# Scores of a pair's two heads issued side by side in the banded attention and both memory attentions

## The chip, the cores and the metric

One core of one Trainium2 chip. The metric is the device time of one execution in microseconds. TensorE (PE) multiplies, VectorE (DVE), ScalarE (ACT) and GpSimd (POOL) work on tiles, SyncE (SP) issues most transfers. PSUM, where products land, has eight banks here, all taken by one kind of tile (`ps`, 128 x 512).

## What is computed

The reference is two blocks on 512 positions of 1024 features, all in float32. The first has a gated long convolution, a chunked mLSTM with 4 heads and a feed-forward. The second has two layers, each followed by a feed-forward: layer A (keys chosen by an indexer, then latent attention) and layer B (banded attention). Both layers add memory attention. Only these matter here, cut down:

```python
B_HEADS, B_KV_HEADS, B_HEAD_DIM, B_WINDOW = 16, 4, 64, 128
MEM_LEN, MEM_HEADS, MEM_HEAD_DIM = 256, 4, 64

# layer B: query i sees keys j with 0 <= i - j < 128; four query heads share a key/value head
s = einsum('bnqhgd,bnkhd->bnhgqk', qb, kk) * scale
s = where(mask, s, NEG_INF)
m = maximum(max(s, -1), sk)                # sk: a learned sink of each head
p = exp(s - m[..., None])
p = p / (sum(p, -1) + exp(sk - m))[..., None]
o = einsum('bnhgqk,bnkhd->bnqhgd', p, vv)

# memory attention, in both layers, 256 keys
s = einsum('bshd,bmhd->bhsm', q, k) * MEM_HEAD_DIM ** -0.5
o = einsum('bhsm,bmhd->bshd', softmax(s, -1), v)
x = x + concatenate([mix, mem_o], -1) @ w_out
```

## The kernel before

Every product is done as three TensorE matmuls of rounded parts (high x high, high x low, low x high), in the function `mm3` (lines 356 to 358). An operand's parts are made by a cast on ScalarE (L347) and a subtraction on VectorE (L348); weights by a cast on ScalarE (L337) and a subtraction on VectorE or GpSimd (L340).

A head has 64 dims, so two heads share the 128 partitions: head e = 0 is in rows 0 to 63, head e = 1 in rows 64 to 127. A score product uses 64 rows of TensorE. In layer B, `pairs_b` is called for each half of the 16 heads: four pairs, eight heads. For one head, `first` makes four score pieces (128 queries by 128 or 256 keys) in two `ps` tiles and then the softmax: VectorE adds the mask and takes the maximum (L1600, one for each piece), joins the sink (L1604), ScalarE does four exponentials (L1607) and the sink's (L1610), VectorE adds and inverts (L1611, L1613), GpSimd scales four pieces (L1615). `second` transposes seven pieces of 128 x 128 (L490) into two `ps` tiles, splits them (`pt`, L347 and L348), multiplies with the values (`head_out`, L1179 to L1186 and `mm3`) into one `ps` tile for the pair, and splits that after the pair's second head. `mem_attn` does the same for four heads with 256 keys: two tiles of scores for a head, reduce (L1206), exponentials (L1213, two for a tile), reciprocal (L1216), scaling (L1219).

The order of the code is written by generators. `pipe(n, first, second, ahead)` runs `first` for `ahead` heads (3 in `pairs_b` and in layer A's memory attention, 1 in layer B's), then `second` of a head and `first` of a later one in turn. `weave` mixes the steps of such a chain with those of a projection: in layer B's first half with the queries of the second half and the memory queries (1.2 steps for each), in the second half, where `both` also mixes `pairs_b` and `mem_attn`, with the output projection `b_wo` (0.4 steps). From that code a scheduler makes the final order of each engine's instructions; an engine works through its own in order.

Of the kernel before, what the change touches and what calls it, by code (L numbers as in the profile page):

```python
# [8 lines left out]
ALU = mybir.AluOpType  # L9
# [26 lines left out]
# ---------------------------------------------------------------- host layout  # L36
# [179 lines left out]
# ---------------------------------------------------------------- the kernel  # L216
class Net:
# [17 lines left out]
    # ---- tiles  # L235
# [20 lines left out]
    # ---- background work, mixed in between weight units: chains of steps, two at a time  # L256
# [15 lines left out]
    # ---- order of emission: pieces of matrix products go between the steps of dependent chains  # L272
# [7 lines left out]
    def weave(self, g, fill, rate=1.0):  # L280
        """Steps of g, each followed by `rate` steps of fill; then the rest of fill."""
# [14 lines left out]
    def pipe(self, n, first, second, ahead=2):  # L296
        """first(i) runs ahead of second(i, what first returned)."""
# [8 lines left out]

    def both(self, a, b):
        """Two steps of a, one of b, and so on."""
# [120 lines left out]
    # ---- norms  # L429
# [16 lines left out]
    def colsum(self, *parts, nb=NB):  # L446
        """Sums over partitions and parts, as columns [position, block]."""
# [7 lines left out]
    def rstd(self, src, n, count, tag="rstd"):  # L455
        """1/sqrt(src/count + EPS) on columns."""
# [15 lines left out]
    def bcast(self, rc, nb=NB, out=None):  # L472
        """Columns [s, block] to a tile [any partition, s]."""
# [18 lines left out]
    # ---- prologue  # L492
    def setup(self):
# [17 lines left out]
        # has the table of the square root loaded in time  # L511
# [27 lines left out]
    def rope_tables(self):  # L539
# [6 lines left out]
        for rot in (32, 16):  # L546
# [13 lines left out]
            # whichever way the conversion rounds, the rest comes into [-pi, pi]  # L560
# [28 lines left out]
    def gain(self, o, k, g):  # L589
        """(1 + scale) * g of a norm, as a column."""  # L590
# [11 lines left out]
    def mod_norm(self, k, bc, aff, shift):  # L602
        """rms_norm(x) * g * (1 + scale) + shift, as two parts."""
# [28 lines left out]
    def conv31(self, out, a, i):  # L632
        """The long convolution, with its input in PSUM."""
# [16 lines left out]
    def block1(self):  # L650
# [28 lines left out]
        # the first n-tiles go along with the modulation, feature tile by feature tile  # L679
# [125 lines left out]
    def gates(self, h):  # L805
        """Input and forget gates: the running maximum of i - F, its columns, and exp(-m)."""
# [35 lines left out]
    def values1(self, h, c):  # L842
        """v of two heads, with a column of ones behind each."""
# [39 lines left out]
    def scores1(self, hd, qk, g):  # L883
# [6 lines left out]
        # where the weights of key block j are: j = 0 | j = 1, 3 | j = 2  # L890
# [219 lines left out]
    def mem_proj(self, layer):  # L1110
        """Keys [2 heads x 64, 256] and values [256, heads], as two parts."""
# [76 lines left out]
    def mem_attn(self, qm, ahead=3):  # L1188
        """qm: 2 x ([128, s] hi, lo)."""
        nc = self.nc  # L1190
        keys, vals = self.mem
        outs = []

        def first(i):
            pr, e = i // 2, 1 - i % 2
            r = slice(64 * e, 64 * e + 64)
            pes = []
# [490 lines left out]
```

## Time and profile before

| | us |
|---|---|
| median of three runs | 2231.48 (2231.43 to 2233.22) |
| span of the profiled execution | 2231.4 |
| layer A, stretch of the memory attention | 1033.5 to 1092.5 |
| layer B, banded and memory attention | 1671.7 to 1818.2 |
| last feed-forward | 1818.2 to the end |

The profile is of one execution; its span is 0.08 us below the median of the runs, inside their spread. Busy time counts an instruction from its start to its end, and TensorE's matmuls overlap each other, so distances from start to start tell more there. A wait is shown with the instruction that released it.

### The profile page before, as it was taken

Reading aid. Unit: us, or ns where it says so; the run is one execution under the profiler, and the core shown is the slowest. Engines: PE = TensorE matmul, PEld = TensorE weight load, DVE = VectorE, ACT = ScalarE, POOL = GpSimd, SP = SyncE. Lnnn points to the kernel's source line nnn. Section 1 sums busy time; section 2 is a strip of 40 time slices with the busy share of each in tenths; the row PEclk is TensorE's granted clock in tenths of the full one; section 3 lists DMA queues with packets and bytes.
Section 4 is the critical chain, followed back from the end, with each engine's and each line's share of the span. In section 5 each row is a group of like instructions: output and inputs, shape, how many; then the busy total and the mean of one; then the engine's idle time right before and its main releaser. Section 6 shows DMA issues by size and latency. Waiting matters only on the chain.

```text
span 2231.4 us, 28798 instructions
## 1 busy us (share of the span) xinstructions
PE 2170.9 (97%) x9988; PEld 1752.3 (79%) x9988; DVE 1367.6 (61%) x2677; ACT 996.3 (45%) x1856; POOL 531.2 (24%) x518
## 2 busy tenths in 40 slices
PE   6999999989999999998999999999999999999998
PEld 4888888867788888876778888888887778888886
DVE  8887967596733333669985654545556665545354
ACT  4655457724422323545464432323545645323233
POOL 3554454552000000242451210101133321101010
PEclk9999999999999999999999999999999999999999
DMA  7322222283422222221211222222321012222222
GB/s 264 105 86 81 93 83 90 92 276 126 157 95 95 95 95 95 97 79 43 67 57 62 99 94 94 94 95 94 118 86 53 33 48 90 94 95 94 95 94 88
DMA packets 120534, 216.91 MB, mean 97 GB/s; under 512 B 13762, under 2 KB 18114, under 8 KB 120388
## 3 DMA queue, kind: packets, MB, share of 16 engines
q1 hardware_dynamic: 120388, 215.08, 28.8%
q8 instruction: 78, 1.28, 0.2%
q14 instruction: 68, 0.56, 0.1%
HBM read 212.93 MB, written 2.10 MB: 96 GB/s over the span
## 4 chain that ended last, share of the span: by engine, by line
PE 87%; DVE 8%; issue 2%; DMA 2%; ACT 1%; SPq 0%; POOL 0%; DVEq 0%; ACTq 0%; POOLq 0%
PE ps L356 28%; PE ps L357 28%; PE ps L358 28%; PE ps L490 2%; DVE big L585 2%; DMA big<-in_ada_dram 1%; DVE bias L1434 1%; DVE m L1433 1%; DVE bias L1396 0%; DVE x L1310 0%; DVE rope L1105 0%; PE ps L451 0%; DVE hs L348 0%; DMA x<-in_xT_dram 0%; PE ps L480 0%
## 5 line engine op out<-in xcount | busy, mean ns | idle before, releaser
L337 ACT CAST wh<-st 128x512 fp32r<-128x512 f32 (+1 forms) x698 | 429.2, 617 | 877.1 <-PE ps L357 592.8
L357 PE MATMUL ps<-hs,wh 128*128 128x512 f32 x1800 | 715.2, 397 | 5.3 <-DVE hs L612 5.1
L358 PE MATMUL ps<-hs,wl 128*128 128x512 f32 x1800 | 712.7, 397 | 7.5 <-DVE wl L340 5.1
L356 PE MATMUL ps<-hs,wh 128*128 128x512 f32 x1800 | 711.4, 399 | 5.7 <-ACT hs L611 5.1
L340 DVE TENSOR_TENSOR wl<-st,wh 128x512 fp32r<-128x512 f32 x488 | 346.7, 712 | 302.3 <-ACT wh L337 299.6
L358 PEld LDWEIGHTS ps<-hs,wl 128*128 128x128 f32 x1800 | 339.3, 188 | 91.6 <-DVE wl L340 7.1
L356 PEld LDWEIGHTS ps<-hs,wh 128*128 128x128 f32 x1800 | 339.2, 189 | 91.3 <-ACT hs L611 8.3
L357 PEld LDWEIGHTS ps<-hs,wh 128*128 128x128 f32 x1800 | 339.2, 188 | 88.5 <-DVE hs L612 7.0
L340 POOL TENSOR_TENSOR wl<-st,wh 128x512 fp32r<-128x512 f32 (+1 forms) x210 | 280.9, 1341 | 360.6 <-ACT wh L337 334.5
L1036 POOL TENSOR_TENSOR t<-t,t 128x512 f32<-128x512 f32 x44 | 69.3, 1576 | 602.5 <-DVE t L1035 533.4
L438 POOL TENSOR_TENSOR t<-t,t 128x512 f32<-128x512 f32 (+1 forms) x51 | 64.3, 1261 | 521.6 <-ACT t L434 520.1
L627 DVE SCALAR_TENSOR_TENSOR big<-ps,vec,big 128x511 f32<-128x511 f32 (+28 forms) x240 | 160.9, 719 | 11.3 <-ACT big L624 11.3
L358 PE MATMUL ps<-big,wl 128*128 128x512 f32 x400 | 157.8, 396 | 2.3 <-POOL wl L340 2.3
L356 PE MATMUL ps<-big,wh 128*128 128x512 f32 x400 | 157.8, 396 | 0.0
L357 PE MATMUL ps<-big,wh 128*128 128x512 f32 x400 | 157.7, 395 | 0.0
L357 PE MATMUL ps<-wl,hs 128*128 128x512 f32 (+1 forms) x320 | 125.3, 392 | 0.0
L358 PE MATMUL ps<-wh,hs 128*128 128x512 f32 (+1 forms) x320 | 124.8, 390 | 0.0
L356 PE MATMUL ps<-wh,hs 128*128 128x512 f32 (+1 forms) x320 | 124.0, 394 | 0.0
L348 DVE TENSOR_TENSOR big<-t,big 128x512 fp32r<-128x512 f32 (+1 forms) x86 | 58.6, 689 | 79.3 <-ACT big L347 77.3
L347 ACT CAST big<-t 128x512 fp32r<-128x512 f32 (+1 forms) x86 | 51.4, 600 | 99.4 <-POOL t L1036 83.7
L358 PEld LDWEIGHTS ps<-big,wl 128*128 128x128 f32 x400 | 75.4, 189 | 21.0 <-POOL wl L340 3.1
L357 PEld LDWEIGHTS ps<-big,wh 128*128 128x128 f32 x400 | 75.5, 189 | 17.9
(324 smaller groups left out, 2970.9 us busy)
## 6 DMA issues: line engine op xcount, KB each, us to landing
st<-in_f_up_dram SPq DMA_DIRECT2D x176, 256.0 KB, 2.6
st<-in_w_up_dram SPq DMA_DIRECT2D x88, 256.0 KB, 2.5
st<-in_f_down_dram SPq DMA_DIRECT2D x88, 256.0 KB, 2.6
big<-in_ada_dram SPq DMA_DIRECT2D x80, 256.0 KB, 5.0
st<-in_w_down_dram SPq DMA_DIRECT2D x44, 256.0 KB, 2.5
st<-in_w_qk_dram SPq DMA_DIRECT2D x32, 256.0 KB, 2.5
st<-in_w_ogm_dram SPq DMA_DIRECT2D x32, 256.0 KB, 2.5
st<-in_w_glu_dram SPq DMA_DIRECT2D x20, 256.0 KB, 2.5
```

What stands on the lines that cost most here:

```text
L337: nc.scalar.copy(wh, st)
L340: eng.tensor_tensor(out=wl, in0=st, in1=wh.bitcast(F32), op=ALU.subtract)
L347: nc.scalar.copy(hi, src)
L348: nc.vector.tensor_sub(lo, src, hi.bitcast(F32))
L356: nc.tensor.matmul(out, lh, rh, start=start, stop=False)
L357: nc.tensor.matmul(out, lh, rl, start=False, stop=False)
L358: nc.tensor.matmul(out, ll, rh, start=False, stop=stop)
L438: (add or nc.gpsimd).tensor_tensor(out=acc, in0=acc, in1=sq, op=ALU.add)
L490: self.nc.tensor.transpose(out, in_, self.ident[:p, :p])
L585: nc.vector.tensor_tensor_reduce(out=st, in0=st, in1=self.siluc[half], scale=1.0, scalar=acc, op0=ALU.mult, op1=ALU.add, accum_out=out)
L627: nc.vector.scalar_tensor_tensor(out=out[:, d:], in0=x[:, :S - d], scalar=w(j), in1=out[:, d:], op0=ALU.mult, op1=ALU.add)
L1036: nc.gpsimd.tensor_tensor(out=b, in0=b, in1=hold["a"], op=ALU.mult)
```

## The change

A new function `mm3_rows` takes the score products of two heads and issues their three matmuls in turn. `first` of `pairs_b` and of `mem_attn` now takes a pair: two `ps` tiles, one for each head, are filled in turn, the reduces follow for both, and after half of the pieces there is a step for the weaving. In `pairs_b` the softmax of both heads then follows, head 1 first. `pipe` with its `ahead` gives way to `pipe2`: scores of pair 0, then for each pair `second` of its head 1, `first` of the next pair, `second` of its head 0. In after, `mm3` is at lines 368 to 370, the transposes at L512, split at L359 and L360, unit at L349 and L352, `mm3_rows` at L376, L378 and L380, the exponentials at L1636 and L1238.

```diff
+    def pipe2(self, n, first, second):
+        st = yield from first(0)
+        for pr in range(n):
+            more = first(pr + 1) if pr + 1 < n else None
+            nxt = None
+            for i in range(2):
+                yield from second(2 * pr + i, st[1 - i])
+                if more and i == 0:
+                    nxt = yield from more
+            st = nxt
...
+    def mm3_rows(self, *prods):
+        nc = self.nc
+        for out, lh, ll, rh, rl in prods:
+            nc.tensor.matmul(out, lh, rh, start=True, stop=False)
+        for out, lh, ll, rh, rl in prods:
+            nc.tensor.matmul(out, lh, rl, start=False, stop=False)
+        for out, lh, ll, rh, rl in prods:
+            nc.tensor.matmul(out, ll, rh, start=False, stop=True)
...
     def pairs_b(...):
-        def first(i):
-            pr, e = i // 2, 1 - i % 2
+        def first(pr):
...
                 if j % 2 == 0:
-                    both = self.t()
-                    sc2 = self.ps()
+                    both = [self.t(), self.t()]
+                    sc2 = [self.ps(), self.ps()]
                 w = slice((j % 2) * 256, (j % 2) * 256 + n)
-                sc = sc2[:, w]
-                self.mm3(sc, q[j][0][r, d], q[j][1][r, d], k[0][r, n0:n0 + n], k[1][r, n0:n0 + n],
-                         True, True)
+                rows = [slice(64 * e, 64 * e + 64) for e in (1, 0)]
+                self.mm3_rows(*((sc2[x][:, w], q[j][0][r, d], q[j][1][r, d], k[0][r, n0:n0 + n],
+                                 k[1][r, n0:n0 + n]) for x, r in enumerate(rows)))
...
+                if j == 1:
+                    yield
+            for x, e in enumerate((1, 0)):
...
-        yield from self.pipe(8, first, second, ahead)
+        yield from self.pipe2(4, first, second)
...
     def mem_attn(...):
...
-        yield from self.pipe(4, first, second, ahead)
+        yield from self.pipe2(2, first, second)
```

The numbers of instructions of each engine stay the same. Up to layer A's memory attention the order of every engine stays too, and again in the last feed-forward.

The order at three places of layer B. First TensorE at the first scores of the first half: `ps_15180` and `ps_15190` (before) are head 1, `ps_15234` and `ps_15244` head 0; in after 15181 and 15219 are head 1, 15182 and 15220 head 0; `big` are keys, `q` queries, `ps_15103` a projection. Before:

```order
L356 MATMUL ps_15180<-big_14966,q_15146 128x128
L357 MATMUL ps_15180<-big_14967,q_15146 128x128
L358 MATMUL ps_15180<-big_14966,q_15147 128x128
L356 MATMUL ps_15190<-big_14966,q_15164 128x256
L357 MATMUL ps_15190<-big_14967,q_15164 128x256
L358 MATMUL ps_15103<-wh_15268,hs_14579 128x512
L358 MATMUL ps_15190<-big_14966,q_15165 128x256
L356 MATMUL ps_15234<-big_14966,q_15146 128x128
L357 MATMUL ps_15234<-big_14967,q_15146 128x128
L358 MATMUL ps_15234<-big_14966,q_15147 128x128
L356 MATMUL ps_15244<-big_14966,q_15164 128x256
L357 MATMUL ps_15244<-big_14967,q_15164 128x256
```

After:

```order
L376 MATMUL ps_15181<-big_14966,q_15146 128x128
L378 MATMUL ps_15181<-big_14967,q_15146 128x128
L380 MATMUL ps_15181<-big_14966,q_15147 128x128
L376 MATMUL ps_15182<-big_14966,q_15146 128x128
L378 MATMUL ps_15182<-big_14967,q_15146 128x128
L380 MATMUL ps_15182<-big_14966,q_15147 128x128
L376 MATMUL ps_15219<-big_14966,q_15164 128x256
L378 MATMUL ps_15219<-big_14967,q_15164 128x256
L380 MATMUL ps_15219<-big_14966,q_15165 128x256
L376 MATMUL ps_15220<-big_14966,q_15164 128x256
L378 MATMUL ps_15220<-big_14967,q_15164 128x256
L380 MATMUL ps_15220<-big_14966,q_15165 128x256
```

One burst of twelve score products stands where a projection's product interrupted it, and a pair's two heads have their tiles filled for the same pieces. Next TensorE at the transposes of pair 1's first head (`t_15287`, `t_15297` before; `t_15335`, `t_15373` after). Before, its own last score product is 64 matmuls ahead of the first transpose; `ps_15546` are scores of later heads, `ps_15374` is values times weights of pair 0, `hs` are queries of the next half:

```order
L356 MATMUL ps_15546<-big_14975,q_15173 128x256
L357 MATMUL ps_15546<-big_14976,q_15173 128x256
L358 MATMUL ps_15546<-big_14975,q_15174 128x256
L357 MATMUL ps_15374<-pt_15451,big_14834 64x256
L358 MATMUL ps_15374<-pt_15450,big_14835 64x256
L356 MATMUL ps_15374<-pt_15454,big_14864 64x256
L490 MATMUL ps_15569<-cst,hs_15484 128x128 x4
L490 MATMUL ps_15578<-cst,t_15287 128x128 x3
L490 MATMUL ps_15578<-cst,t_15297 128x128
L490 MATMUL ps_15579<-cst,t_15297 128x128 x3
```

After; the burst with the last scores of `t_15373` ends 16 matmuls ahead of its first transpose, three transposes of queries and twelve products with values come between, the last six of which are shown:

```order
L368 MATMUL ps_15320<-pt_15450,big_14849 64x256
L369 MATMUL ps_15320<-pt_15451,big_14849 64x256
L370 MATMUL ps_15320<-pt_15450,big_14850 64x256
L1201 MATMUL ps_15320<-pt_15454,big_14879 64x128
L1202 MATMUL ps_15320<-pt_15455,big_14879 64x128
L1205 MATMUL ps_15320<-pt_15454,big_14880 128x128
L512 MATMUL ps_15533<-cst,t_15335 128x128 x3
L512 MATMUL ps_15533<-cst,t_15373 128x128
L512 MATMUL ps_15534<-cst,t_15373 128x128
L512 MATMUL ps_15550<-cst,hs_15484 128x128 x4
L512 MATMUL ps_15534<-cst,t_15373 128x128 x2
L368 MATMUL ps_15559<-pt_15542,big_14834 128x256
```

The distance to a head's scores went from 64 matmuls to 16, and the first product with the transposed weights (`pt_15542`) stands directly behind the transposes. Last, ScalarE at pair 0 of the second half (`t_15981`, `t_15991` before, `t_15981`, `t_16001` after: head 1; `t_16017`, `t_16027` before, `t_15982`, `t_16002` after: head 0; L1213 and L1238: memory attention). Before:

```order
L1607 ACTIVATE t_15981,l_3739_15980<-t_15981,m_3738_15979 128x128
L1607 ACTIVATE t_15981,l_3739_15980<-t_15981,m_3738_15979 128x256
L1607 ACTIVATE t_15991,l_3739_15980<-t_15991,m_3738_15979 128x256 x2
L1610 ACTIVATE es_3744_16006<-m_3738_15979,sk_14621 128x4
L347 CAST hs_15975<-ps_15933 128x512
L1607 ACTIVATE t_16017,l_3747_16016<-t_16017,m_3746_16015 128x128
L1607 ACTIVATE t_16017,l_3747_16016<-t_16017,m_3746_16015 128x256
L1607 ACTIVATE t_16027,l_3747_16016<-t_16027,m_3746_16015 128x256 x2
L1610 ACTIVATE es_3752_16042<-m_3746_16015,sk_14621 128x4
L1213 ACTIVATE t_16080,l_3761_16079<-ps_16069,mx_3760_16076 128x256 x2
L337 CAST wh_16485<-st_16484 128x512
L347 CAST pt_16152<-ps_16143 128x512
```

After:

```order
L1636 ACTIVATE t_16001,l_3748_16021<-t_16001,m_3738_15979 128x256 x2
L1639 ACTIVATE es_3749_16027<-m_3738_15979,sk_14621 128x4
L359 CAST hs_15975<-ps_15933 128x512
L1636 ACTIVATE t_15982,l_3751_16036<-t_15982,m_3739_15980 128x128
L1636 ACTIVATE t_15982,l_3751_16036<-t_15982,m_3739_15980 128x256
L1636 ACTIVATE t_16002,l_3751_16036<-t_16002,m_3739_15980 128x256 x2
L1639 ACTIVATE es_3752_16042<-m_3739_15980,sk_14621 128x4
L1238 ACTIVATE t_16069,l_3757_16068<-ps_16051,mx_3756_16065 128x256 x2
L1238 ACTIVATE t_16080,l_3761_16079<-ps_16052,mx_3760_16076 128x256 x2
L349 CAST wh_16503<-st_16502 128x512
L359 CAST pt_16116<-ps_16107 128x512
```

The cast of head 1's first transposed tile (`pt_16152` before, `pt_16116` after) stands behind one memory piece more.

## Rows read from the trace of the kernel before

**Rows 1.** The page, busy time by engine (part 1) and the chain that ended last (part 4).
```profile
PE 2170.9 (97%) x9988; PEld 1752.3 (79%) x9988; DVE 1367.6 (61%) x2677; ACT 996.3 (45%) x1856; POOL 531.2 (24%) x518
...
PE 87%; DVE 8%; issue 2%; DMA 2%; ACT 1%; SPq 0%; POOL 0%; DVEq 0%; ACTq 0%; POOLq 0%
```

**Rows 2.** Windows: stretch, length, then busy time of each engine, granted clock.
```profile
1033.50:1092.50 59.00, 54.26 (x268) 42.89 (x267) 58.70 (x162) 26.76 (x66) 21.32 (x29) 0.97 0.12 41
1671.70:1818.20 146.50, 143.03 (x851) 114.00 (x849) 92.98 (x297) 84.73 (x258) 47.78 (x88) 1.00 0.12 39
1818.20:1860.00 41.80, 41.80 (x181) 33.51 (x180) 24.63 (x31) 18.84 (x32) 9.09 (x7) 1.00 0.28 92
```

**Rows 3.** Timeline of TensorE: start, duration, line, tile; two score bursts of layer B.
```profile
1709.22 0.40 PE L358 MATMUL ps<-hs,wl 128*128 128x512 f32 x1
1709.54 0.38 PE L356 MATMUL ps<-big,q 64*128 64x256 f32 x1
...
1711.40 0.40 PE L358 MATMUL ps<-hs,wl 128*128 128x512 f32 x1
```

**Rows 4.** Timeline of TensorE, the indexer's scores; x2 are two that start together.
```profile
993.55 0.39 PE L356 MATMUL ps<-big,q 64*128 64x256 f32 x2
...
994.25 0.28 PE L358 MATMUL ps<-big,q 64*128 64x256 f32 x2
```

**Rows 5.** Timeline of TensorE near the end of layer B.
```profile
1805.09 0.28 PE L356 MATMUL ps<-pt,big 128*64 128x256 f32 x1
1805.20 0.28 PE L357 MATMUL ps<-pt,big 128*64 128x256 f32 x1
...
1805.56 0.22 PE L1185 MATMUL ps<-pt,big 128*64 128x128 f32 x1
1805.62 0.28 PE L1186 MATMUL ps<-pt,big 128*128 128x128 f32 x1
...
1808.26 0.39 PE L356 MATMUL ps<-pt,big 128*128 128x256 f32 x1 [1.57 <-ACT pt L347]
1808.48 1.36 PE L490 MATMUL ps<-cst,t 128*128 128x128 f32 x11
1809.60 0.37 PE L357 MATMUL ps<-pt,big 128*128 128x256 f32 x1
```

**Rows 6.** Timeline of TensorE: a head's last score product and its first transpose.
```profile
1729.29 0.28 PE L358 MATMUL ps<-big,q 64*128 64x256 f32 x1
...
1734.10 0.33 PE L490 MATMUL ps<-cst,t 128*128 128x128 f32 x1
```

**Rows 7.** Timeline of VectorE, the same head.
```profile
1729.25 0.42 DVE L1600 CUSTOM_DVE_ANT_0 t<-ps,cst 128x256 f32<-128x256 f32 x1 [0.53 <-PE ps L358]
...
1729.68 0.42 DVE L1600 CUSTOM_DVE_ANT_0 t<-ps,cst 128x256 f32<-128x256 f32 x1
...
1733.33 0.18 DVE L1613 RECIPROCAL rl<-l 128x4 f32<-128x4 f32 x1
```

**Rows 8.** Timeline of ScalarE: the same head, then a memory piece, then a cast.
```profile
1730.86 0.40 ACT L1607 ACTIVATE t<-t,m 128x128 f32<-128x128 f32 x1 [0.39 <-DVE m L1604]
...
1732.75 0.28 ACT L1610 ACTIVATE es<-m,sk 128x4 f32<-128x4 f32 x1
...
1741.45 0.47 ACT L1213 ACTIVATE t<-ps,mx 128x256 f32<-128x256 f32 x1 [3.80 <-DVE mx L1208]
...
1742.37 0.39 ACT L1607 ACTIVATE t<-t,m 128x128 f32<-128x128 f32 x1
...
1749.16 0.59 ACT L347 CAST pt<-ps 128x512 fp32r<-128x512 f32 x1 [0.70 <-PE ps L490]
```

**Rows 9.** Timeline of GpSimd, the same head.
```profile
1733.67 1.74 POOL L1615 TENSOR_SCALAR t<-t,rl 128x128 f32<-128x128 f32 x4 [1.57 <-DVE rl L1613]
```

**Rows 10.** TensorE's wait for the memory queries, then the window behind it.
```profile
1040.55 0.38 PE L356 MATMUL ps<-big,q 64*128 64x256 f32 x1 [2.56 <-DVE t L1251]
...
1041.90:1045.30 3.40, 3.40 (x10) 2.62 (x9) 3.40 (x9) 0.72 (x2) 0.00 (x0) 0.50 0.02 5
```

**Rows 11.** Waits of TensorE in layer B: line, releaser, us, times, longest.
```profile
PE ps L356 <- ACT pt L347: 1.9, 2, 1.6
```

More of the change, by code (lines that the diff above doesn't have):

```diff
@@ L1221, in first @@
-                pes.append(pe)
+                    rows = [slice(64 * e, 64 * e + 64) for e in (1, 0)]
+                    self.mm3_rows(*((scs[n][:, i * MEM:(i + 1) * MEM], qm[pr][0][r, c],
+                                     qm[pr][1][r, c], keys[pr][0][r, :], keys[pr][1][r, :])
+                                    for n, r in enumerate(rows)))
+                for n, e in enumerate((1, 0)):
+                    sc = scs[n]
+                    mx = self.sm(2, "mx2")
+                    nc.vector.tensor_reduce(out=mx, in_=sc.rearrange("p (i m) -> p i m", i=2),
+                                            axis=AX.X, op=ALU.max)
+                    nc.vector.tensor_scalar(out=mx, in0=mx, scalar1=-0.125, scalar2=None,
+                                            op0=ALU.mult)
+                    l = self.sm(2, "l2")
+                    pe = self.t()
+                    for i in range(2):
+                        c = slice(i * MEM, (i + 1) * MEM)
+                        nc.scalar.activation(out=pe[:, c], in_=sc[:, c], func=AF.Exp, scale=0.125,
+                                             bias=mx[:, i:i + 1], accum_out=l[:, i:i + 1])
+                    rl = self.sm(2, "rl2")
+                    nc.vector.reciprocal(rl, l)
+                    for i in range(2):
+                        c = slice(i * MEM, (i + 1) * MEM)
+                        nc.gpsimd.tensor_scalar(out=pe[:, c], in0=pe[:, c], scalar1=rl[:, i:i + 1],
+                                                scalar2=1.0, op0=ALU.mult, op1=ALU.mult)
+                    pes[e].append(pe)
@@ L1222, in first @@
+                if half == 0:
+                    yield
             yield
@@ L1571, in layer_b, with pairs_b @@
         self.run_all(self.proj_out("b_wo", 4, mo + second))
-    def pairs_b(self, q, kT, vs, half, sk, ahead):
+    def pairs_b(self, q, kT, vs, half, sk):
         nc = self.nc
@@ L1578, in pairs_b, with first @@
         hold = {}
-        def first(i):
-            pr, e = i // 2, 1 - i % 2
-            hd = 8 * half + 2 * pr + e
+        def first(pr):
             k = kT[2 * half + pr // 2]
-            r = slice(64 * e, 64 * e + 64)
             d = slice(pr * P, (pr + 1) * P)
-            m4 = self.sm(NB, "m4")
-            l4 = self.sm(NB, "l4")
-            pes = []
+            m4 = [self.sm(NB, "m4") for _ in range(2)]
+            pes = {1: [], 0: []}
             for j in range(NB):
@@ L1603, in first @@
-                pes.append(both[:, w])
-            nc.vector.tensor_scalar(out=m4, in0=m4, scalar1=sk[:, hd:hd + 1], scalar2=-1.0,
-                                    op0=ALU.max, op1=ALU.mult)
-            for j in range(NB):
-                nc.scalar.activation(out=pes[j], in_=pes[j], func=AF.Exp, bias=m4[:, j:j + 1],
-                                     accum_out=l4[:, j:j + 1])
-            es = self.sm(NB, "es4")
-            nc.scalar.activation(out=es, in_=m4, func=AF.Exp, bias=sk[:, hd:hd + 1])
@@ L1611, in first @@
-            nc.vector.tensor_add(l4, l4, es)
-            rl = self.sm(NB, "rl4")
-            nc.vector.reciprocal(rl, l4)
-            for j in range(NB):
-                nc.gpsimd.tensor_scalar(out=pes[j], in0=pes[j], scalar1=rl[:, j:j + 1], scalar2=1.0,
-                                        op0=ALU.mult, op1=ALU.mult)
+                rows = [slice(64 * e, 64 * e + 64) for e in (1, 0)]
+                self.mm3_rows(*((sc2[x][:, w], q[j][0][r, d], q[j][1][r, d], k[0][r, n0:n0 + n],
+                                 k[1][r, n0:n0 + n]) for x, r in enumerate(rows)))
@@ new lines, in first @@
+                for x, e in enumerate((1, 0)):
+                    nc.vector.tensor_tensor_reduce(out=both[x][:, w], in0=sc2[x][:, w], in1=bm,
+                                                   scale=scale, scalar=LOWEST, op0=ALU.add,
+                                                   op1=ALU.max, accum_out=m4[x][:, j:j + 1])
+                    pes[e].append(both[x][:, w])
+                if j == 1:
+                    yield
+            for x, e in enumerate((1, 0)):
+                hd = 8 * half + 2 * pr + e
+                m, l4 = m4[x], self.sm(NB, "l4")
+                nc.vector.tensor_scalar(out=m, in0=m, scalar1=sk[:, hd:hd + 1], scalar2=-1.0,
+                                        op0=ALU.max, op1=ALU.mult)
+                for j in range(NB):
+                    nc.scalar.activation(out=pes[e][j], in_=pes[e][j], func=AF.Exp, bias=m[:, j:j + 1],
+                                         accum_out=l4[:, j:j + 1])
+                es = self.sm(NB, "es4")
+                nc.scalar.activation(out=es, in_=m, func=AF.Exp, bias=sk[:, hd:hd + 1])
+                nc.vector.tensor_add(l4, l4, es)
+                rl = self.sm(NB, "rl4")
+                nc.vector.reciprocal(rl, l4)
+                for j in range(NB):
+                    nc.gpsimd.tensor_scalar(out=pes[e][j], in0=pes[e][j], scalar1=rl[:, j:j + 1],
+                                            scalar2=1.0, op0=ALU.mult, op1=ALU.mult)
```

34 lines of the change are left out of this document (6 added, 28 removed).

## The prediction

> **What bounds the kernel now.** Read the page's totals and its chain first, then the stretches, then single rows. TensorE is busy 97% of the span and is 87% of the chain that ended last [rows 1]. The change touches two stretches. In layer A's memory attention (1033.5 to 1092.5 us) VectorE is busy 58.70 of 59.00 us and TensorE 54.26: VectorE sets the end there, with the top-k work of the indexer. In layer B (1671.7 to 1818.2 us) TensorE is busy 143.03 of 146.50 us, VectorE only 92.98 and ScalarE 84.73; behind it the feed-forward keeps TensorE busy 41.80 of 41.80 us [rows 2]. So what layer B wins or loses on TensorE moves the end by the same amount, and what layer A wins on TensorE is hidden by VectorE.
>
> The busy time of rows overlaps (matmuls are pipelined), so I cost by start-to-start distances. A 512-wide product takes 0.232 us; two bursts of three 64-row score products between three such products take 1709.22 to 1711.40, 2.18 us, where 3 x 0.232 + 6 x 0.117 = 1.40 would do: a burst of 64-row products costs 0.39 us on top of its products [rows 3]. A 256-wide product takes 0.117 us, a 128-wide one into 64 columns 0.06, a transpose about 0.105 (eleven in 1.12) [rows 5].
>
> Layer B has, in either kernel, 254 products 512 wide, 144 of 256 and 50 of 128 (0.232, 0.117, 0.0585 us: 78.6), 160 transposes (at 0.109, the distance of single ones: 17.4) and 240 score products (192 of 0.117 and 48 of 0.111: 27.8). Before, the scores lie in 46 bursts (18.0), and 17 pairs of them lie beside each other already (-2.0). That is 139.8 us; the stretch took 146.5. So 6.7 us are waits of TensorE, the largest one for a cast of ScalarE [rows 11].
>
> **The change part by part.** No product and no step of a softmax is removed; every engine has the same instructions.
>
> *Overlap.* The trace has a place where 64-row products of both row halves stand together: twelve, from 993.55 to 994.25, all in pairs that start together, a pair each 0.117 us [rows 4]. So a pair costs as much as one product. Layer B can have 120 pairs; in the new order 106 fall into one burst, 17 did: 89 x 0.117 = 10.3 us less. Before, the program issued that burst at 993.55 three and three, not in turn, and it overlapped all the same, so I count every pair in a burst.
>
> *Fewer bursts.* 30 where 46 were: 16 x 0.39 = 6.3 us less. Together 16.6 us, all on the path, since TensorE sets the end there.
>
> The Trainium skill ("TensorEngine Tiling (Array Packing)", Key Properties) says that changing the tiling mode drains TensorE. For the 64-row bursts rows 3 agree, with 0.39 us. For tiles of 64 columns they don't: at 1805.56 a product into 64 columns is followed by one into 128 after 0.06 us [rows 5]. By the rule the borders of 64-column tiles, 46 before and 38 after, would count too; at half of 0.39 each the 16.6 us would be 18.2.
>
> *The pipeline.* What is moved is the distance between a head's scores and its transposes. Before, scores ran three heads ahead. Now both heads of a pair get their scores together, and the next pair's scores go between the two heads. What lies between is the softmax: VectorE adds the mask and takes the maximum, ScalarE does four exponentials and the sink's, VectorE inverts the sum, GpSimd scales four pieces, then TensorE transposes.
>
> The trace has the length of that chain for one head with nothing else in the way: last score at 1729.29 (done about 0.2 later), reduces from 1729.25, exponentials from 1730.86 to 1733.03 (2.17 us), reciprocal 1733.33, GpSimd 1733.67, first transpose 1734.10 [rows 6 to 9]: 4.6 us. With two heads in one burst VectorE has two more reduces of 0.43 us ahead of the maximum: 5.5 us for the first head. The second head's exponentials stand behind the first's: 7.7 us. GpSimd gives a scaled piece each 0.44 us (four in 1.74 [rows 9]) where TensorE could transpose two: a head that is waited for costs 1.0 us more until its last piece.
>
> The Trainium skill (same page, PSUM Bottleneck) says that tiling speeds up TensorE but not the emptying of PSUM. Rows 4 and 7 agree: six pairs take 0.7 us, the four tiles they fill take VectorE 1.7. Without the two queued reduces the waits below would be 4 to 5 us less.
>
> Against 5.5 us stands the other work that the order puts between. In layer B's second half, memory attention's exponentials (0.92 us for a half of a head [rows 8]) also stand in ScalarE's queue. The six places with less than 5.5 us (counted in the order of the changed kernel, pieces of which stand in the section on the change):
> - pair 1 of the first half: 12 products of head values and three transposes, 2.1 us: wait 3.4, scaling 1.0, and the first product needs a cast that stands behind the second head's exponentials, 1.0. Together 5.4.
> - pair 3 of the first half: 2.0 us of other work: 3.5 + 1.0, the cast 0.5, then the second head follows at once (7.7 less what has passed, 0.6, and 0.5 of scaling): 6.1.
> - second half, pair 0: 4.3 us: 1.2. Then the product right behind the transposes needs the cast of them (0.59), which stands on ScalarE behind the second head's exponentials (2.2), a split's cast (0.46), two memory pieces (1.8) and a weight cast (0.46). Before it stood there too, but TensorE had other work first. From the end of the first head's exponentials the cast is done after 5.5; TensorE comes there after 2.3: 3.2. Together 4.4.
> - pair 1: 2.7 us: 2.8, two casts ahead 1.0, scaling 0.9: 4.7.
> - pair 2: 4.6 us: 0.9, scaling 0.9, again a cast behind exponentials, 2.2: 4.0.
> - pair 3: 2.6 us: 2.9 + 1.0, cast 0.5, second head 1.0: 5.4.
>
> That is 30.0 us, and 0.8 at the end of the last pair, as before. What stands behind the waiting product on TensorE waits too, since it works in order: weights' products of the output projection most of all. The pairs that are left have 7 to 17 us of other work and wait for nothing. All other engines get slower by it, not busier.
>
> *Layer A.* Its four heads: 49.9 us of TensorE work before, 49.8 after (four bursts become five, more overlap). VectorE bounds the stretch, and its instructions are the same: 0. TensorE idles 4.74 of the 59.00 us [rows 2]; some half of that, 2 us either way, I allow for the order of VectorE's work.
>
> **Sum.** -16.6 + (30.8 - 6.7) = +7.5 us. The profiled execution has a span of 2231.4 us, the median of the three runs is 2231.48: they can be taken as one. 2231.4 + 7.5 = 2239 us.
>
> **Rivals.**
> 1. *Faster: the waits stay near those of before.* Evidence for it: the head of rows 6 had 3.7 us of other work ahead of its transposes and cost a wait of only about 1.2, and the longest wait of layer B for a cast was 1.6 us [rows 11]; while TensorE waits, the others catch up. If the chain stays 4.6 us and neither casts nor scaling bite, the six places cost 2.5 + 2.6 + 0.3 + 1.9 + 0 + 2.0 = 9.3 us: -16.6 + 9.3 - 6.7 = -14.0, 2217 us. Against it: the two reduces and the exponentials are in the queue's order ahead of the casts and cannot be passed.
> 2. *About the same.* The chain is 5.5 us and scaling counts, but the casts find ScalarE free: 4.4 + 5.1 + 2.1 + 3.7 + 1.8 + 4.4 = 21.5; -16.6 + 21.5 - 6.7 = -1.8: 2230 us.
> 3. *Slower, the clock falls.* After a wait of 2.56 us at 1040.55 (for the memory queries) the granted clock was 0.50 for 3.4 us from 1041.90 [rows 10], that is 1.2 GHz for 2.4. Such a stretch costs up to 1.7 us. Of the waits above four are over 2.8 us; three or four falls give +6: 2245 us. It counts from the first wait that is about as long as that one; the wait of 1.57 us at 1808.26 [rows 5] had no fall behind it, since layer B's clock is 1.00 [rows 2].
> 4. *The change does not do what it says: the halves don't overlap.* Then only 6.3 us are won, and the same waits come: 2239 + 10.3 = 2249 us. Against it: rows 4.
>
> **How the numbers follow.** Likeliest is the sum with its waits, 2239 us: 0.34. Clock on top 0.10, no overlap 0.06: with these, slower by over 0.2% (4.5 us; about what a measurement of this kernel can tell from no change) has 0.50. Rival 2: same, 0.22. Rival 1: faster, 0.28. The range reaches from rival 1 (2217) to rival 4 (2249), which leaves out gains of over 14 us (about 0.1) and several falls of the clock on top of all waits (under 0.1). For the cases slower alone it would be 2236 to 2250.
>
> **What would show it.** In the profile after, layer B's score products start in pairs, as those of rows 4, and there are 30 bursts of them; if they start 0.117 us apart one by one, rival 4 holds. TensorE's waits in layer B for GpSimd's scaled pieces (the transposes) and for ScalarE's casts sum to about 30 us where they were some 3 in that view; near 10 means rival 1. TensorE's busy time in layer B falls, and the stretch is longer than 146.5 us. The granted clock in layer B was 1.00; 0.50 in stretches of 3.4 us means rival 3. Layer A ends where it did, within 2 us. I would be wrong if the second pair's scores or the output projection fill more of the six places than the order shows, or if ScalarE's queue empties faster than 2.2 us a head.

## The result, and the profile after

The median of the changed kernel is 2256.86 us (2256.45 to 2260.1) against 2231.66 (2231.43 to 2233.22) for the kernel before, timed beside it: a ratio of 1.0112 [1.0099, 1.0124], 25.2 us slower. The sign is that of the forecast, the size is not: 2239.0 had been named, and 2256.86 lies above the range, 2217 to 2249. The profiled execution has a span of 2258.4 us.

The page of after, its busy time and its chain, to be laid beside [rows 1]:

```profile
PE 2176.7 (96%) x9988; PEld 1756.7 (78%) x9988; DVE 1364.9 (60%) x2677; ACT 996.3 (44%) x1856; POOL 531.1 (24%) x518
...
PE 86%; DVE 8%; ACT 2%; issue 2%; DMA 2%; SPq 0%; POOL 0%; DVEq 0%; ACTq 0%; POOLq 0%
```

TensorE has the same 9988 matmuls and is busy for 5.8 us longer, although more of them overlap. That is the first hint that something beside waits is at work. In the chain ScalarE has 2% where it had 1%. The windows say where (stretch, length, busy time of PE, PEld, DVE, ACT, POOL, granted clock, DMA share, GB/s): layer A's memory attention, layer B, the last feed-forward, as in [rows 2]:

```profile
1037.90:1096.90 59.00, 50.84 (x248) 39.25 (x247) 56.50 (x156) 23.06 (x60) 19.84 (x27) 0.94 0.13 41
1676.30:1845.00 168.70, 146.47 (x852) 116.80 (x851) 91.95 (x297) 84.31 (x258) 46.51 (x88) 0.88 0.10 34
1845.00:1886.80 41.80, 41.80 (x181) 33.51 (x180) 24.52 (x31) 19.05 (x32) 9.08 (x7) 1.00 0.28 94
```

Layer B grew from 146.5 to 168.7 us, the feed-forward behind it is the same. From the start of layer A's memory attention to that of layer B passed 638.2 us before and 638.4 after, so in these two profiles layer A gives and takes nothing. In layer B two numbers moved: TensorE stands idle for 168.70 - 146.47 = 22.2 us (3.5 before), and the granted clock is 0.88 (1.00 before). VectorE, ScalarE and GpSimd have the work they had.

The waits of TensorE in layer B, as a sum (line, releaser, us, times, longest):

```profile
PE ps L512 <- POOL t L1644: 12.7, 5, 3.2
PE ps L368 <- ACT pt L359: 5.7, 3, 2.7
PE ps L369 <- DVE pt L360: 2.5, 2, 2.0
PE ps L368 <- ACT hs L359: 0.7, 1, 0.7
```

and the long ones singly, from TensorE's timeline (the idle time ahead of the instruction, and its releaser, in brackets):

```profile
1697.58 0.38 PE L368 MATMUL ps<-pt,big 128*128 128x256 f32 x1 [1.56 <-ACT pt L359]
...
1701.40 0.58 PE L369 MATMUL ps<-pt,big 128*128 128x256 f32 x1 [1.97 <-DVE pt L360]
...
1710.72 1.35 PE L512 MATMUL ps<-cst,t 128*128 128x128 f32 x5 [2.40 <-POOL t L1644]
...
1742.18 2.06 PE L512 MATMUL ps<-cst,t 128*128 128x128 f32 x7 [3.00 <-POOL t L1644]
...
1761.53 0.58 PE L368 MATMUL ps<-pt,big 128*128 128x256 f32 x1 [2.75 <-ACT pt L359]
...
1781.46 1.60 PE L512 MATMUL ps<-cst,t 128*128 128x128 f32 x5 [3.23 <-POOL t L1644]
...
1804.82 2.06 PE L512 MATMUL ps<-cst,t 128*128 128x128 f32 x7 [1.45 <-POOL t L1644]
...
1808.29 0.58 PE L368 MATMUL ps<-pt,big 128*128 128x256 f32 x1 [1.41 <-ACT pt L359]
...
1828.70 2.06 PE L512 MATMUL ps<-cst,t 128*128 128x128 f32 x7 [2.57 <-POOL t L1644]
```

In order of time these are pairs 0 (two), 1 and 3 of the first half and pairs 0, 1, 2 (two) and 3 of the second. Most releasers are the two that were forecast: scaled pieces of GpSimd ahead of transposes, and casts of ScalarE; at 1701.40 it is a subtraction of VectorE. The durations at the left show the rest: seven transposes take 2.06 us at 1742.18, where eleven took 1.36 in [rows 5], and a 256-wide product 0.58 instead of 0.39. The windows of the six places where the granted clock was low (columns as above):

```profile
1699.90:1706.70 6.80, 5.30 (x29) 4.86 (x30) 4.98 (x22) 0.64 (x2) 0.00 (x0) 0.50 0.10 35
1740.90:1751.10 10.20, 8.91 (x41) 6.89 (x41) 4.90 (x17) 4.84 (x16) 3.48 (x8) 0.50 0.00 0
1761.40:1768.20 6.80, 6.67 (x19) 4.80 (x19) 2.08 (x7) 0.69 (x3) 1.77 (x3) 0.51 0.12 41
1781.80:1785.20 3.40, 3.28 (x10) 2.63 (x11) 1.71 (x4) 1.68 (x6) 2.72 (x7) 0.51 0.00 0
1805.70:1812.50 6.80, 5.37 (x24) 4.35 (x24) 4.54 (x13) 4.84 (x15) 4.43 (x9) 0.50 0.10 39
1829.60:1836.40 6.80, 6.73 (x25) 5.61 (x26) 2.19 (x5) 2.23 (x6) 2.15 (x5) 0.50 0.00 1
sum 40.80, PE 36.25 PEld 29.14 DVE 20.40 ACT 14.92 POOL 14.56; mean PE 6.04 PEld 4.86 DVE 3.40 ACT 2.49 POOL 2.43
```

For 40.8 us the granted clock was 0.50, that is 1.2 instead of 2.4 GHz. Each stretch begins within a wait of the list above, or less than a us behind one.

How well the halves overlap is seen at layer B's first burst (x2: two that start together):

```profile
1680.74 0.39 PE L369 MATMUL ps<-wl,hs 128*128 128x512 f32 x1
1681.06 0.33 PE L376 MATMUL ps<-big,q 64*128 64x128 f32 x2
1681.23 0.28 PE L378 MATMUL ps<-big,q 64*128 64x128 f32 x2
1681.34 0.28 PE L380 MATMUL ps<-big,q 64*128 64x128 f32 x2
1681.45 0.34 PE L376 MATMUL ps<-big,q 64*128 64x256 f32 x2
1681.62 0.29 PE L378 MATMUL ps<-big,q 64*128 64x256 f32 x2
1681.74 0.29 PE L380 MATMUL ps<-big,q 64*128 64x256 f32 x2
1681.96 0.50 PE L370 MATMUL ps<-wh,hs 128*128 128x512 f32 x1
1682.30 0.40 PE L368 MATMUL ps<-wh,hs 128*128 128x512 f32 x1
```

Six pairs, each at the price of one product: from 1680.74 to 1682.30 pass 1.56 us, two 512-wide products and six of 0.117 are 1.17, so the burst costs 0.39 on top, as forecast.

**The sum, made again.** In layer B: 101 pairs start together where 14 did, 87 x 0.117 = -10.2; 30 bursts where 46 were, -6.3; idle time +18.7; low clock: a 512-wide product takes 0.427 us there instead of 0.232 (from start to start; rows below), so, as an estimate, of 36.25 busy us 36.25 x (1 - 0.232/0.427) = 16.6 are lost. Together +18.8 of 22.2 us; the other 3.4 aren't assigned (perhaps delays too small to show as idle time, because records overlap; no run shows it). Of the 25.2 us between the medians some 3 aren't in layer B. In this profile layer A's attention started 4.4 us later, behind work whose order hasn't changed; over the profiles of all kernels that start moves by -1.6 to +4.6 us, and the time at low clock ahead of it is 10.2 to 27.3 us (13.7 before, 23.9 after). What the median has of that is left open.

### The profile page after: what moved, and what is told of

Read it like the earlier page. It is cut to its first block, busy times and chain, and to the rows that moved or that the text cites. A ratio compares the mean times of both kernels' runs of the same rounds, so it can differ in the third digit from the quotient of the medians.

```text
span 2258.4 us, 28792 instructions
## 1 busy us (share of the span) xinstructions
PE 2176.7 (96%) x9988; PEld 1756.7 (78%) x9988; DVE 1364.9 (60%) x2677; ACT 996.3 (44%) x1856; POOL 531.1 (24%) x518
## 4 chain that ended last, share of the span: by engine, by line
PE 86%; DVE 8%; ACT 2%; issue 2%; DMA 2%; SPq 0%; POOL 0%; DVEq 0%; ACTq 0%; POOLq 0%
PE ps L368 28%; PE ps L369 27%; PE ps L370 27%; PE ps L512 2%; DVE big L607 1%; DMA big<-in_ada_dram 1%; ACT t L1636 1%; DVE bias L1423 1%; DVE bias L1461 1%; DVE m L1460 1%; DVE rope L1127 1%; PE ps L376 0%; DVE x L1337 0%; PE ps L502 0%; PE ps L473 0%
## 5 line engine op out<-in xcount | busy, mean ns | idle before, releaser
L349 ACT CAST wh<-st 128x512 fp32r<-128x512 f32 (+1 forms) x698 | 429.1, 617 | 893.8 <-PE ps L369 605.0
L352 DVE TENSOR_TENSOR wl<-st,wh 128x512 fp32r<-128x512 f32 x488 | 346.3, 711 | 302.9 <-ACT wh L349 300.6
L352 POOL TENSOR_TENSOR wl<-st,wh 128x512 fp32r<-128x512 f32 (+1 forms) x210 | 280.6, 1340 | 376.0 <-ACT wh L349 348.1
L360 DVE TENSOR_TENSOR big<-t,big 128x512 fp32r<-128x512 f32 (+1 forms) x86 | 58.6, 688 | 79.4 <-ACT big L359 77.4
L359 ACT CAST big<-t 128x512 fp32r<-128x512 f32 (+1 forms) x86 | 51.4, 601 | 99.0 <-POOL t L1058 83.7
```

The costliest lines, as they stand in the source:

```text
L349: nc.scalar.copy(wh, st)
L352: eng.tensor_tensor(out=wl, in0=st, in1=wh.bitcast(F32), op=ALU.subtract)
L359: nc.scalar.copy(hi, src)
L360: nc.vector.tensor_sub(lo, src, hi.bitcast(F32))
```

## The experiments

Theories as they stand in the expectations. **A**: the shortened distance between scores and transposes makes waits, and behind them the clock is low; both cost time, and nothing else does. **B**: products in pairs lower the clock by themselves. **C**: the chain of the softmax sets the time of layer B, and the low clock only fills up its waits. The stretches were cut at the same instructions in every profile:

| kernel | median us | layer B us | TensorE idle | low clock us | pairs together | bursts |
|---|---|---|---|---|---|---|
| before | 2231.66 | 146.5 | 3.5 | 0 | 14 | 46 |
| after | 2256.86 | 168.7 | 22.2 | 40.8 | 101 | 30 |
| after_again | 2258.9 | 168.6 | 22.2 | 40.8 | 101 | 30 |
| e2_mem_only | 2235.8 | 148.4 | 4.8 | 3.4 | 29 | 44 |
| e3_pairs_only | 2249.58 | 161.5 | 17.4 | 23.9 | 72 | 34 |
| e8_distance_only | 2255.38 | 165.7 | 16.7 | 34.1 | 40 | 30 |
| e1_fill | 2255.15 | 166.8 | 5.2 | 17.1 | 90 | 39 |
| e5_fill2 | 2247.99 | 158.7 | 3.5 | 0 | 90 | 39 |
| e4_soft_split | 2230.4 | 142.0 | 5.8 | 6.8 | 70 | 39 |
| e7_woven | 2226.53 | 138.6 | 3.5 | 3.4 | 85 | 36 |

Pairs are score products that start within 20 ns of each other in the trace. Layer B, idle time, low clock, pairs and bursts are of one profile each. Ratios below are against the kernel before on the same chip (2232.56 to 2233.31).

**One part alone.** e2_mem_only keeps the new form in both memory attentions and has `pairs_b` as before; e3_pairs_only the other way round.

```diff
 # e2_mem_only, in pairs_b
-        yield from self.pipe2(4, first, second)
+        yield from self.pipe(8, first, second, ahead)
 # e3_pairs_only, in mem_attn
-        yield from self.pipe2(2, first, second)
+        yield from self.pipe(4, first, second, ahead)
```

> Only the memory attentions by pairs; banded attention as before the change, three heads ahead. Theory A: the long waits were in the banded attention, so layer B's waits are back near the 3.6 us (over 0.5 us each) of before, no half clock there; 18 more pairs of products overlap (2 us) and two bursts fewer: 2227 to 2234 us. If the memory part alone brought waits (its exponentials stand in ScalarE's queue ahead of casts): 2236 to 2245.

> Only the banded attention by pairs; memory attentions as before the change. Theory A: most of the loss is here: 2248 to 2256 us, waits of 18 to 24 us in layer B and half clock behind the longest. If the loss came from memory's exponentials standing in the queues: 2231 to 2240.

e2: 1.0010 [1.0001, 1.0019], 2235.8 us, just above what A expected and just under its rival; layer B has 4.8 us of idle time and one fall of the clock, where A had expected none. e3: 1.0072 [1.0058, 1.0085], 2249.58 us, as expected, with 17.4 us of idle time. The memory attentions alone change little; `pairs_b` alone brings 15.0 of layer B's 22.2 us. Both together have 5.3 more than the sum of 1.9 and 15.0; one reason is seen in ScalarE's timeline further on, where exponentials of both kinds stand ahead of the cast that TensorE waits for.

**The distance alone.** e8_distance_only keeps the new pipe but issues a pair's scores head by head, as single products.

```diff
-            for j in range(NB):
...
-                self.mm3_rows(*((sc2[x][:, w], q[j][0][r, d], q[j][1][r, d], k[0][r, n0:n0 + n],
-                                 k[1][r, n0:n0 + n]) for x, r in enumerate(rows)))
+            for x, e in enumerate((1, 0)):
+                r = slice(64 * e, 64 * e + 64)
+                for j in range(NB):
...
+                    self.mm3(sc2[:, w], q[j][0][r, d], q[j][1][r, d], k[0][r, n0:n0 + n],
+                             k[1][r, n0:n0 + n], True, True)
```

> The change's pipeline (both heads of a pair, then the next pair between their values) with the banded scores not side by side: all pieces of head 1, then all of head 0, each product by itself; memory attentions as in the change. If the distance alone makes the loss, the waits of layer B are again some 20 us with half clock behind them: 2250 to 2262 us, a little over the changed kernel, since less overlaps. If the side by side order had a cost of its own (PSUM tiles of two heads held at once, the reduces of both in one queue), this is faster than the changed kernel: 2240 to 2250.

1.0106 [1.0090, 1.0121], 2255.38 us: with 40 pairs instead of 101, nearly the whole loss of after. It is inside the range, but not over the changed kernel (2258.9 us on the same chip), as had been expected. The window of its layer B and the two largest sums of waits:

```profile
1674.00:1839.70 165.70, 149.01 (x851) 121.19 (x850) 92.62 (x297) 84.25 (x258) 47.66 (x88) 0.90 0.11 34
```

```profile
PE ps L368 <- ACT pt L359: 9.2, 5, 3.0
PE ps L512 <- POOL t L1644: 5.4, 2, 3.0
```

Most of the waits and of the low clock (34.1 us) come with the distance and without the pairs. That speaks against B, and for A. A part goes with the pairs all the same: 61 fewer of them should cost 7.1 us, but the stretch is 3.0 us shorter than after's, with 5.5 us less idle time and 6.7 us less of low clock, and waits for scaled pieces are 5.4 us where after has 12.7.

**The waits filled.** e1_fill puts 512-wide products whose results are not read where TensorE waits, 85 of them in all, 19.7 us of extra work; most pairs stay, and little idle time is meant to be left for the clock to fall behind.

```diff
+FILL = {(0, 0): (0, 14), (0, 1): (10, 0), (0, 3): (12, 0), (1, 0): (0, 12), (1, 1): (14, 0),
+        (1, 2): (6, 6), (1, 3): (11, 0)}
...
+            for _ in range(fill[0]):
+                self.nc.tensor.matmul(pts[0], vs[0][0][:, 0:P], vs[0][0][:, 0:S], start=True, stop=True)
...
+            for _ in range(fill[1]):
+                self.nc.tensor.matmul(o, vs[0][0][:, 0:P], vs[0][0][:, 0:S], start=True, stop=True)
```

> The changed kernel with 85 extra products, 512 wide (0.232 us each at full clock, 19.7 us in all), whose results nothing reads, put ahead of the transposes or of the value products at the seven places of layer B where TensorE waited 1.8 to 3.5 us. Theory A (a wait costs twice: itself, and the lower clock behind it): the extra products stand in waits that are there anyway, TensorE idles little, the granted clock of layer B stays near 1.00, and the some 18 us that its 41 us at 0.50 cost come back: 2240 to 2250 us although there is more work. Rival B (the paired 64-row products themselves bring the clock down): the clock falls as before, and the time is 2257 or up to 2277. Rival C (the softmax chain sets the time, the low clock only filled what would have been wait): clock near 1.00, but the time stays at 2254 to 2260.

1.0095 [1.0079, 1.0111], 2255.15 us: A's 2240 to 2250 is missed, and the time is C's. The trace says why that doesn't decide it yet: layer B's clock is 0.95, not near 1.00. The extra products of pair 3 in the first half had nothing to hold them back and ran early, between score products; one long wait was left, with the longest stretch of low clock of all kernels behind it. The filling also moved others of TensorE's instructions, and bursts rose from 30 to 39 (+3.5 us). First TensorE's timeline, then the windows of layer B and of that stretch:

```profile
1740.93 1.80 PE L514 MATMUL ps<-cst,t 128*128 128x128 f32 x7 [2.56 <-POOL t L1646]
...
1756.36 0.79 PE L370 MATMUL ps<-hs,wh 128*128 128x512 f32 x1
...
1757.38 0.63 PE L372 MATMUL ps<-hs,wl 128*128 128x512 f32 x1
1757.81 0.63 PE L370 MATMUL ps<-hs,wh 128*128 128x512 f32 x1
1758.23 0.63 PE L371 MATMUL ps<-hs,wh 128*128 128x512 f32 x1
```

```profile
1672.20:1839.00 166.80, 161.62 (x936) 127.11 (x934) 92.95 (x297) 83.95 (x258) 46.92 (x88) 0.95 0.11 34
1743.40:1760.50 17.10, 16.99 (x76) 13.70 (x76) 8.29 (x33) 7.68 (x29) 4.14 (x11) 0.50 0.00 1
```

One wait of 2.56 us was followed, 2.5 us after its end, by 17.1 us at a granted clock of 0.50, in which TensorE was busy for 16.99 us. The last three rows of the timeline give the price of a 512-wide product there, 0.427 us from start to start. Everywhere else in layer B the clock was full. A's terms give this kernel too: 19.7 us of work, 17.0 less idle time, 8.8 less lost at low clock (16.99 x 0.457 = 7.8 for 16.6), 3.5 for bursts and 1.3 for 11 pairs fewer are -1.3 against after; measured are -1.9.

**Filled, and held in place.** In e5_fill2 the extra products ahead of transposes read the previous head's cast, so they can't start early. (73 are 384 wide and 32 are 512 wide, some 20 us; the expectation says 85 of 384.)

```diff
+            for _ in range(fill[0]):
+                z = hold["z"]
+                self.nc.tensor.matmul(pts[0][:, :3 * P], z[:, 0:P], z[:, :3 * P], start=True, stop=True)
...
+            hold["z"] = pp[1][0]
```

> As the first filled kernel (which still had one wait of 2.8 us at pair 3 and a stretch of 17.1 us at half clock behind it), but the extra products ahead of transposes read the last cast of the head before, so that they cannot start early: 105 products, 85 of them 384 wide and the rest 512 wide, some 21 us at full clock. Theory A: no wait over 1 us is left, no half clock in layer B, and against the changed kernel the 22 us of waits are replaced by 21 us of work while 41 us at half clock (some 16 us of loss) go; 9 more bursts and 10 pairs fewer cost 4.5 us: layer B some 12 us shorter, 2243 to 2250 us on this chip. Rival C (the chain sets the time): the place of the half clock is taken by more small waits, 2254 to 2260 us.

1.0069 [1.0055, 1.0083], 2247.99 us: inside A's range, outside C's. The window of layer B, and the largest wait that is left in it:

```profile
1671.50:1830.20 158.70, 155.19 (x956) 124.14 (x955) 92.43 (x297) 83.77 (x258) 47.26 (x88) 1.00 0.11 36
```

```profile
PE ps L514 <- POOL t L1646: 1.0, 1, 1.0
```

TensorE does 20 us more work than in after and layer B is 10.0 us shorter; the granted clock is 1.00 with 90 pairs. B falls: pairs don't lower the clock. C says that layer B couldn't have become shorter. Worked out, e5 gives 10.0 us net, pays 3.5 for nine bursts more, 1.3 for 11 pairs fewer, and 1.3 because the filling is that much more than the idle time it replaces (20.0 against 18.7): 16.1 us for the low clock, beside the 16.6 of the sum above. This is no measurement of the clock alone, since the filling moved other instructions too. e1 and e5 lie closer to each other. Here are the two rows of e5 that answer those of e1 at 1740.93 and 1756.36; between them TensorE has the same instructions in the same order in both, and nothing of the filling:

```profile
1737.79 1.81 PE L514 MATMUL ps<-cst,t 128*128 128x128 f32 x7 [0.98 <-POOL t L1646]
...
1747.83 0.50 PE L370 MATMUL ps<-hs,wh 128*128 128x512 f32 x1
```

The same work takes 10.04 us in e5 and 15.43 in e1, where 12.9 us of it have the low clock: 5.4 us are lost with next to no idle time in the stretch. That is the price of the clock by itself, and C falls.

**The distance given back.** e4_soft_split keeps scores in pairs, but has one pair's scores issued ahead of the other's transposes and splits the softmax off: each head's exponentials are issued behind the transposes and splits of the pair ahead of it, so that casts don't queue behind them. Layer B's memory pieces have buffers of another kind.

```diff
+        got = yield from first(0)
+        soft(0, 1, got)
+        yield
+        soft(0, 0, got)
+        for pr in range(4):
+            nxt = None
+            if pr < 3:
+                nxt = yield from first(pr + 1)
+            for e in (1, 0):
+                pp = turn(pr, e, got[0][e])
+                if nxt:
+                    soft(pr + 1, e, nxt)
+                yield
+                value(pr, e, pp)
+            got = nxt
```

> Scores of a pair's heads side by side as in the change, but the distance put back: the next pair's scores come ahead of this pair's transposes, and its softmax is issued head by head between this pair's transposes and value products, so a cast no longer stands behind both heads' exponentials; layer B's memory weights take the free q tiles. 80 pairs overlap (17 before), 39 bursts (46). Theory A: waits of layer B near 10 us, few or no stretches at half clock; 7.4 us less for overlap, 2.7 for bursts, some 4 to 7 more wait: 2222 to 2232 us. Rival B (pairs lower the clock): half clock remains, 2240 or more.

0.9989 [0.9980, 0.9997], 2230.4 us, as expected: 70 pairs (80 had been named) and 39 bursts, idle time 5.8 us. The window of layer B and its two largest waits:

```profile
1674.80:1816.80 142.00, 136.17 (x851) 108.86 (x849) 89.20 (x297) 83.98 (x258) 46.81 (x88) 0.98 0.13 40
```

```profile
PE ps L379 <- ACT pt L370: 2.9, 1, 2.9
PE ps L523 <- POOL t L1660: 1.5, 1, 1.5
```

What is gained against before, 7 bursts and 56 pairs, is 2.7 + 6.6 = 9.3 us; 2.3 of more idle time and two stretches of low clock (6.8 us, at most 3.1 lost) give back 5.4. That leaves -3.9; the stretch is 4.5 us shorter. Which of the two measures does how much, the pair of scores ahead or the exponentials behind the casts, was not tried apart.

e7_woven is e4 with both pairs of a memory attention's scores ahead of its first transposes, one step of `mem_attn` for each step of `pairs_b` where it was one for two, and the weave of the first half with the queries at 1.35 instead of 1.2.

```diff
-        yield from self.pipe2(2, first, second)
+        yield from self.pipe3(2, first, second, 2)
...
-        todo = [a, a, b]
+        todo = [a, b]
...
-        first = self.weave(self.pairs_b(q, kT, vs, 0, sk), rest(), 1.2)
+        first = self.weave(self.pairs_b(q, kT, vs, 0, sk), rest(), 1.35)
```

> As the kernel with the split softmax, with the first half's fill at 1.35 steps for 1.2, banded and memory attention woven one to one in the second half, and both pairs of memory scores issued ahead in both layers. Theory A: no wait of 2 us or more is left in layer B (the split kernel had one of 3.1 and one of 1.8 us, with 6.8 us at half clock behind them), so no half clock there: layer B 4 to 8 us shorter than the split kernel's, 2220 to 2228 us on this chip, faster than before by 0.2 to 0.6%. Rival B (paired products lower the clock, this kernel has more of them): half clock in layer B again, 2230 or more.

0.9971 [0.9961, 0.9981], 2226.53 us: faster than both kernels, and inside the expected 2220 to 2228. Two parts were missed: the stretch is 3.4 us shorter than e4's where 4 to 8 had been named, and one fall of the clock (3.4 us) is left behind a wait of 1.8 us. Layer B of e7, with a single wait of over a us left:

```profile
1673.80:1812.40 138.60, 135.06 (x851) 107.32 (x850) 89.00 (x297) 84.36 (x258) 46.78 (x88) 0.99 0.13 42
```

```profile
PE ps L523 <- POOL t L1660: 2.0, 2, 1.8
```

Idle time is 3.5 us as before the change, and TensorE's busy time is 8.0 us less than in [rows 2]: here the gain of the overlap reaches the end.

**After once more.** The same kernel with no edit, for how far one profile speaks for others.

> The changed kernel again, on this chip and beside the others. Theory A: layer B again takes 165 to 171 us, 30 us and more of it at half clock, and the work ahead of layer A's memory attention, whose order is the same as before, takes 1033 to 1038 us (it was 4.4 us longer in the first profile, which would then be the spread of single executions): 2254 to 2260 us.

1.0112 [1.0096, 1.0129], 2258.9 us, as expected; layer A's attention starts 3.2 us later than before. The window of layer B repeats after's to 0.1 us, in length, busy time and clock:

```profile
1675.20:1843.80 168.60, 146.41 (x851) 116.79 (x850) 91.95 (x297) 84.24 (x258) 46.45 (x88) 0.88 0.11 34
```

The stretches of low clock in layer B aren't chance: in both profiles they come at the same places with the same lengths.

## Why the prediction was right in its sign and wrong in its size

- **What bounds: right.** Layer B's change went to the end in full, layer A's 0 was 0.2.
- **Overlap and bursts: right.** Forecast -10.3 and -6.3; counted -10.2 (101 pairs where 106 were forecast, 14 before where 17 were) and -6.3, with 0.39 us for a burst once more. Rival 4 is out.
- **Waits: right in kind, too high in size.** At the six places 30.0 us were forecast; the list shows 2.40, 3.00, 2.75, 3.23, 2.86 and 2.57, 16.8 in all, where the forecast had 5.4, 6.1, 4.4, 4.7, 4.0 and 5.4. What failed to show are the shares for scaling, for the casts that follow at once, and the 1.2 ahead of pair 0's transposes: without these the forecast was 3.4, 3.5, 3.2, 2.8, 3.1 and 2.9, or 18.9, each within 1.0 us of what came. That choice of terms is made with the result known. The prediction's own sign, some 30 us of waits for scaled pieces and casts, came to 20.9 (12.7 + 5.7 + 2.5). Pair 0 of the first half, of which it said that it waits for nothing, waits 1.56 us for a cast and 1.97 for a subtraction. No exponentials stand in the way there: ScalarE's last end at 1693.2, and ahead of the cast at 1696.94 come weight casts and, from 1694.14, four scalings of the next half's queries (2.40 us); VectorE works on those queries until 1700.7. Idle time rose by 18.7 us; the forecast was 24.1, counted from 6.7 before, of which the trace shows 3.5 as idle time.
- **Pieces of one cause, seen on ScalarE.** ScalarE's timeline at the second half's pair 0: first exponential of the second head, first of the memory pieces, a weight's cast, and only then the cast that TensorE waits for until 1761.53.

```profile
1756.35 0.40 ACT L1636 ACTIVATE t<-t,m 128x128 f32<-128x128 f32 x1
...
1758.55 0.47 ACT L1238 ACTIVATE t<-ps,mx 128x256 f32<-128x256 f32 x1
...
1760.37 0.63 ACT L349 CAST wh<-st 128x512 fp32r<-128x512 f32 x1
1760.87 0.99 ACT L359 CAST pt<-ps 128x512 fp32r<-128x512 f32 x2
```

That is the queue that the prediction listed (2.2 of exponentials, 1.8 of memory pieces, 0.46 for a weight), with nearly the same lengths (2.2, 1.8 and 0.5 us from start to start), and the wait of 2.75 for its 3.2.
- **The clock: the step that failed.** The sum took it at nothing, and rival 3, with a chance of 0.10, at +6: three or four falls of 3.4 us, each costing up to 1.7, from waits about as long as the 2.56 us of [rows 10]. There were six falls, 3.4 to 10.2 us long, 40.8 us together: 16.6 us by the sum, 16.1 by e5. Both the number and the length were too small. TensorE's busy time in layer B, of which the prediction said that it falls, rose by 3.4 us. Falls also followed waits of 1.97 us (with one of 1.56 shortly before) and of 1.45, and in e8 one of 1.22, so the point from which rival 3 was to count was too high; and it was no point at all, since the wait of 2.40 us ahead of 1710.72 has none behind it, nor had the 1.57 us of [rows 5].
- **Why it was sized so.** The 3.4 us of [rows 10] are the length of one fall, and the prediction carried it from one stretch to another. In layer B the clock stayed low for up to three times as long, in e1 for five times. Further waits inside a fall don't explain it: TensorE was busy for 16.99 of e1's 17.1 us, and ahead of layer A after has a fall of 6.8 us (1024.0 to 1030.8) without any idle time in it. With 16.6 in place of 0 the forecast would have read 2239 + 16.6 = 2255.6. That it comes so near 2256.86 is partly luck: waits were forecast 5.4 us too long, and against that stand 3.4 us of layer B and some 3 of the median that no term covers.

The Trainium skill ("TensorE: Matmul & The Clock Gate", HAM oscillation — how this bites in real kernels) describes a kernel whose clock falls at each wait between groups of matmuls, so that the cost is paid again and again, and puts it at 1 - 1.2/2.4 of the throttled time. The trace agrees that it comes back: behind six of the nine waits listed. 16.6 of 40.8 us is 0.41, under that half, because TensorE was idle for 4.6 us of the stretches and a 512-wide product takes 0.427 us there, less than twice 0.232.

Not settled: why some waits have a fall behind them and others not, what makes a fall last 3.4 us at one place and 17.1 at another, and the 3 us of the median that layer B doesn't hold.

## What to carry to other kernels

Row halves that are issued side by side do overlap, two for one; but they bring both heads' scores at the same time, so the first transposes come a whole softmax sooner and casts stand behind twice the exponentials: keep the distance (another pair of scores ahead, the exponentials issued behind the casts), and the gain is real, as e7 shows. Where TensorE bounds a stretch and gets several waits of a us or more, cost the low clock behind them as well, and not by the length of a single fall seen elsewhere: here that term was as large as the whole gain. A kernel with the waits filled by products that nobody reads, held in place, tells the cost of the clock from that of the waits.

## What was not expected of the hardware

The granted clock stayed at 0.50 for 3.4 to 17.1 us behind single waits of 1.22 to 3.23 us (in e2 behind three short ones, 1.9 us together), while TensorE was busy again, and single waits of 1.57 and 2.40 us had no fall behind them. Products that nobody reads, put into the waits, made a stretch 10.0 us shorter though they are 20 us of work. In the two profiles of the changed kernel the falls of layer B agree to 0.1 us, counted from its start, while the start of layer A's attention, behind stages whose order is the same, moves by up to 6 us between the profiles of all kernels.
